# Moving the first head pair's projections ahead of the values' stage, and new ratios for merging attention with projections, in a one-core decoder layer

## The chip, the cores and the metric

One core of a Trainium2 chip runs the whole kernel. The metric is the time of one execution in device microseconds, the median of repeated runs; three runs of the kernel before took 2665.83, 2668.41 and 2672.25 us. One more execution was recorded by the hardware profiler, and all numbers of single instructions come from that one.

## The reference, cut to what matters

The layer takes a residual stream x of 1024 tokens by 1024 channels in float32 and applies four blocks, each with a norm ahead and behind: a SwiGLU feed-forward half, a mixer, a cross-attention to 256 memory tokens and a second feed-forward half. The change lies in the mixer, in its first half:

```
proj = u @ w_in
q, k, v, z, xs, bm, cm, dt_raw = split(proj)
# stick-breaking attention, 16 heads of 64, strictly causal:
zz = (q @ k.T) / 8
suffix = reverse_cumsum(log_sigmoid(-zz)) - log_sigmoid(-zz)
a = exp(log_sigmoid(zz) + suffix)          # s < t only
o_att = rmsnorm(a @ v)
# beside it a state-space scan of 16 heads over xs, bm, cm, dt gives o_ssd
m = concat([o_att, o_ssd]) @ w_out
```

## The kernel before

Float32 products are made on TensorE from a high part and a low part of each operand, three matmuls for one (line 279, `mm3`). A projection of one 128-column weight tile over one half of the tokens (512) is 8 x 3 matmuls (line 286, `proj`), accumulated in one bank of a PSUM pool "mm" of three.

**Order of the work.** TensorE's order is written out by hand: every matmul is made to follow the one that the program lists before it (line 100, `_pe`), and a clock of estimated costs runs along. Other engines follow their own lists, ordered by a scheduler that knows the program order as a priority. Some steps are put down with a due time on that clock (line 122, `run_later`) and are listed when TensorE's order has come that far. `merge` (line 156) interleaves two generators so that their shares of two given times, `ta` and `tb`, advance together.

**Weights** come through `wstream` (line 255), one tile ahead of its use: by a transfer on SP, from a copy already split in DRAM where there is one, or raw into "wraw" (two buffers) and then split by ScalarE (high part) and VectorE (low part). High and low parts have three buffers each. A transfer on SP that waits for a buffer holds up all behind it on that queue; POOL's queue works in the same way.

**The stage ahead** is the state-space scan (line 1188, `ssd`). Its last work is `keys` (line 1478), eight tiles of the memory's keys, whose results pass through a buffer "ko" of the tag "Bt" (one buffer) on their way to DRAM.

**Attention** (line 1578) begins with `value_rows` (line 1894): in two halves of the output columns, eight token blocks accumulate in eight PSUM banks at once over four weight tiles. At the end of a half ScalarE reads each bank out, POOL's queue shifts the block by one token, VectorE takes the difference of neighbours, both are split into a buffer of the tag "v" (four buffers), and POOL's queue stores it to DRAM. `differ` and `store` are listed 6.0 and 8.5 us after the block's matmuls on the planner's clock. In DRAM the values lie by head, so that a block's store writes pieces of 512 bytes.

Then the heads go in eight pairs. `inproj(p)` (line 1630) makes queries, keys and loads values of pair p: two projections for the queries (both token halves), two for the keys; each result is split and taken by small row transfers on SP (128 KB each) into operands where a head's high and low parts lie one above the other ("q", "k", and "QL" for the queries' low part). `units(p)` (line 1818) makes the products: for two heads and four groups of 256 queries, `scores` (line 1710: two matmuls per part, a sigmoid on ScalarE, a scan along the keys on VectorE), and one group later `values` (line 1812: transposes on TensorE, a split by ScalarE and VectorE into "ath" and "atl", four buffers each, and matmuls with the values, up to three behind). Pair 0's `inproj` runs alone; then each pair's `units` is merged with the next pair's `inproj`:

```
self.run_all(inproj(0))
for p in range(7):
    self.merge(units(p), 24000, inproj(p + 1), 32500)
self.merge(tail(), 26000, beside(), 21000 + 5200 * MIXED)
```

In the last `inproj`, `before` (line 1692) also loads and scales tiles of the scan's output for the output projection. `tail` is the last pair's products; `beside` is the first part of the output projection and then the memory's values. After that `mix_out` (line 1975) loads the attention's output ("oraw") and squares and sums it.

## Time and profile before

| | us |
|---|---|
| median of three runs | 2668.41 |
| profiled execution | 2669.86 |
| its span | 2667.9 |
| values' stage, first matmul after the keys to last | 1026.3 to 1116.8 |
| pair 0's projections, alone | 1116.8 to 1138.6 |
| products of pair 0 with projections of pair 1 | 1155.6 to 1201.7 |
| one pair of the middle | 50.3 |
| products of the last pair begin | about 1505 |

How to read it: the table's stages are read off the times at which the matmuls of each stage start. The profile gives each engine's busy time, the clock granted to TensorE and the share of the time in which the 16 DMA engines were busy. A row of a timeline has start, duration, engine, line of the code, operation, result and operands; in brackets stands the idle time of the engine just before it, and what ended it. A row of stretches has the length, then for TensorE, its weight loads, VectorE, ScalarE and POOL the busy time with the count of instructions, then granted clock, DMA share and GB/s. A row of DMA issues ends with the size of one and the median time from issue to landing. A row of waits has the total, the count and the longest.

### The profile page before, as it was taken

What the parts mean: (1) busy time and instruction counts of PE and PEld (TensorE: products, weight loads), DVE (VectorE), ACT (ScalarE), POOL (GpSimd) and SP (SyncE); (2) the same over time, 40 slices, a digit from 0 to 9 for tenths busy, and PEclk for the clock granted to TensorE, in tenths of its full rate; (3) what the DMA queues carried; (4) which work ended last, traced back from release to release, by engine and by line L of the source; (5) the groups of instructions that cost most, each with busy time, mean ns of one, the idle gap of its engine ahead of it and who ended that gap; (6) DMA issues with size and microseconds to landing.
All of it is one profiled execution on the core that took longest, in us unless ns stands there. A gap on an engine that the chain in (4) does not pass through costs nothing.

```text
span 2667.9 us, 36670 instructions
## 1 busy us (share of the span) xinstructions
PE 2592.1 (97%) x12786; PEld 2152.1 (81%) x12786; DVE 1941.8 (73%) x2928; ACT 1289.4 (48%) x2232; POOL 662.8 (25%) x822
## 2 busy tenths in 40 slices
PE   9899999999999999979999999999999999999999
PEld 7788888778777788868888787888878788888887
DVE  6778897778689783357777776767565888776767
ACT  6434444555356563345565555346554433333554
POOL 2555553110100001412222210101011555552000
PEclk9999999999999999989999999999999999999999
DMA  6458888774655223775554646637648443236554
GB/s 224 163 193 276 284 282 293 261 248 164 229 184 180 87 79 123 224 193 130 145 148 119 178 129 225 219 128 241 225 150 298 164 166 127 89 105 217 193 166 155
DMA packets 211049, 493.74 MB, mean 185 GB/s; under 512 B 27568, under 2 KB 35888, under 8 KB 210864
## 3 DMA queue, kind: packets, MB, share of 16 engines
q1 hardware_dynamic: 155408, 357.42, 40.2%
q0 software_dynamic: 32128, 91.51, 11.4%
q10 hardware_dynamic: 23328, 42.48, 4.2%
q8 instruction: 100, 1.64, 0.2%
q14 instruction: 85, 0.70, 0.1%
HBM read 327.46 MB, written 138.67 MB: 175 GB/s over the span
## 4 chain that ended last, share of the span: by engine, by line
PE 67%; issue 16%; DVE 7%; DMA 6%; ACT 2%; POOL 1%; SPq 1%; DVEq 0%; ACTq 0%; POOLq 0%
PE mm L138 32%; PE dn L138 28%; PE z L138 2%; DVE nb L1730 1%; PE tr L141 1%; PE ms L138 1%; PE ms L141 1%; PE tr L138 1%; DMA wraw<-in_w_dn 1%; DMA raw<-xs 1%; DMA raw<-in_w_dn 1%; DVE atl L1783 1%; DVE hl L267 1%; DMA oraw<-mix 1%; DMA wraw<-xs 0%
## 5 line engine op out<-in xcount | busy, mean ns | idle before, releaser
L138 PE MATMUL mm<-xh,whi 128*128 128x512 f32 x1192 | 469.9, 404 | 3.9 <-ACT xh L265 2.7
L138 PE MATMUL mm<-xl,whi 128*128 128x512 f32 (+1 forms) x1124 | 438.9, 390 | 5.4 <-DVE xl L267 4.2
L138 PE MATMUL mm<-xh,wlo 128*128 128x512 f32 x1144 | 439.0, 392 | 0.0
L138 PEld LDWEIGHTS mm<-xh,whi 128*128 128x128 f32 x1192 | 225.4, 189 | 45.4 <-ACT xh L265 3.9
L138 PEld LDWEIGHTS mm<-xh,wlo 128*128 128x128 f32 x1144 | 215.3, 188 | 46.8 <-DVE wlo L267 0.4
L138 PEld LDWEIGHTS mm<-xl,whi 128*128 128x128 f32 x1124 | 212.7, 189 | 39.5 <-DVE xl L267 6.3
L1730 DVE TENSOR_TENSOR_SCAN nb<-nb,begin 128x128 f32<-128x128 f32 (+7 forms) x128 | 169.9, 1350 | 52.6 <-ACT nb L1726 52.3
L267 DVE TENSOR_TENSOR wlo<-wraw,whi 128x1024 fp32r<-128x1024 f32 x78 | 95.2, 1221 | 85.1 <-ACT whi L265 84.8
L265 ACT CAST whi<-wraw 128x1024 fp32r<-128x1024 f32 (+1 forms) x95 | 92.3, 972 | 112.8 <-PE mm L138 54.5
L1726 ACT ACTIVATE nb<-z,scale 128x128 f32<-128x128 f32 (+2 forms) x192 | 106.1, 582 | 68.4 <-PE z L138 68.1
L657 ACT ACTIVATE ft<-ft 128x512 f32<-128x512 f32 x88 | 55.5, 632 | 101.1 <-DVE ft L656 100.5
L138 PE MATMUL dn<-xh,wlo 128*128 128x512 f32 x296 | 101.3, 390 | 0.0
L740 POOL TENSOR_TENSOR wc<-wraw,raw 128x512 f32<-128x512 f32 x56 | 80.3, 1434 | 65.1 <-DVE whi L267 17.9
L1782 ACT ACTIVATE ath<-tr,small 128x512 fp32r<-128x512 f32 (+1 forms) x106 | 68.2, 645 | 57.2 <-PE tr L141 53.9
L740 POOL TENSOR_TENSOR wc<-raw,wraw 128x512 f32<-128x512 f32 x55 | 81.1, 1475 | 51.5 <-DVE blk L267 21.6
L138 PE MATMUL z<-k,q 128*128 128x128 f32 (+2 forms) x192 | 67.1, 353 | 26.0 <-DMA k<-dg 16.9
L1783 DVE SCALAR_TENSOR_TENSOR atl<-tr,ath 128x512 fp32r<-128x512 f32 (+1 forms) x106 | 65.7, 625 | 36.2 <-ACT ath L1782 35.4
L825 POOL TENSOR_TENSOR ft<-ft,e 128x512 f32<-128x512 f32 x37 | 59.7, 1614 | 121.4 <-DVE e L824 45.1
L138 PE MATMUL mm<-ath,v 128*128 128x256 f32 x320 | 89.2, 301 | 0.1
L138 PE MATMUL dn<-xh,blk 128*128 128x512 f32 x264 | 85.2, 389 | 0.0
L138 PE MATMUL mm<-atl,v 128*128 128x256 f32 x320 | 83.5, 283 | 0.5 <-DVE atl L1783 0.5
L265 ACT CAST wlo<-wc 128x512 fp32r<-128x512 f32 x79 | 49.1, 621 | 70.8 <-PE dn L138 28.1
(602 smaller groups left out, 6992.2 us busy)
## 6 DMA issues: line engine op xcount, KB each, us to landing
whi<-dwhi SPq DMA_DIRECT2D x74, 512.0 KB, 3.6
wlo<-dwlo SPq DMA_DIRECT2D x74, 512.0 KB, 4.7
wraw<-in_w_gu SPq DMA_DIRECT2D x43, 512.0 KB, 3.9
raw<-in_w_gu SPq DMA_DIRECT2D x37, 512.0 KB, 4.1
wraw<-xs SPq DMA_DIRECT2D x56, 256.0 KB, 3.0
xs<-ft ACTq DMA_DIRECT2D x54, 256.0 KB, 3.3
raw<-xs SPq DMA_DIRECT2D x54, 256.0 KB, 3.2
act<-ft ACTq DMA_DIRECT2D x52, 256.0 KB, 2.3
```

Of the source, the lines that this page charges most:

```text
L138: self._pe(self.nc.tensor.matmul(out, lhsT, rhs, start=start, stop=stop, skip_group_check=self.more), cost)
L141: self._pe(self.nc.tensor.transpose(out, src, self.ident if ident is None else ident), 109.0)
L265: self.kp(self.nc.scalar.copy(hi, src))
L267: self.nc.vector.tensor_tensor(out=lo, in0=src, in1=hi.bitcast(F32), op=ALU.subtract)
L657: nc.scalar.activation(t, t, AF.Silu)
L740: nc.gpsimd.tensor_tensor(out=t, in0=a, in1=b, op=op)
L825: nc.gpsimd.tensor_tensor(out=t1, in0=t1, in1=e, op=ALU.mult)
L1726: nc.scalar.activation(nb[:, s0:s1], z[:, 0:n], AF.Sigmoid, scale=sc[:, i : i + 1])
L1730: nc.vector.tensor_tensor_scan(out=nb[:, 0:Wd][:, ::-1], data0=nb[:, 0:Wd][:, ::-1], data1=begin[:, S - Wd : S][:, ::-1], initial=0.0, op0 ...
L1782: nc.scalar.activation(hi, x, AF.Identity, bias=self.minus)
L1783: nc.vector.scalar_tensor_tensor(out=lo, in0=x, scalar=-1.0, in1=hi.bitcast(F32), op0=ALU.add, op1=ALU.subtract)
```

## The change

- The weight stream hands out query tile 0 and key tile 1 of the first pair ahead of the values' tiles, and key tile 1 again behind them.
- `inproj(0)` makes the queries and the first half of the keys, then calls `value_rows`, then makes the second half of the keys with the tile that came again. The value buffers of a pair are taken when they are loaded. The second set of "QL" is made and cleared behind the values.
- The values lie in DRAM by token block: a block's store writes whole rows of 4 KB, and a head's load reads pieces of 512 bytes. Blocks 5 to 7 are read out into "ath" and "atl" buffers instead of "k".
- The last two tiles of the memory's keys use the tag "csr" instead of "Bt".
- `merge` gets other times: 24900 (20240 for pair 0) to 20740 (21600 for the last), and 32500 for the tail.
- The tiles that `before` loads have two buffers of their own ("mraw"), and a load is listed two steps ahead of its use; the last projection gives way once more before its end.

```diff
--- before.py
+++ after.py
@@ -1491,7 +1491,7 @@
                         nc.vector.tensor_tensor(out=t, in0=ps, in1=rm, op=ALU.mult)
                     i = n % 2
                     if i == 0:
-                        env["ko"] = self.t(sp, [P, 4, MEM], F32R, "Bt")
+                        env["ko"] = self.t(sp, [P, 4, MEM], F32R, "Bt" if n < 6 else "csr")
                     o = env["ko"]
                     self.split(o[:, i, :], o[:, 2 + i, :], t)
                     if i == 1:
@@ -1500,7 +1500,8 @@
             env = {}
             W = self.W = self.wstream(
                 [self.wsrc("ssd", i % 6 if i < 12 else i) for i in range(26)] + [self.wsrc("kv", i) for i in range(8)]
-                + [ap["w_v"][i] for i in range(8)] + [self.wsrc("qk", i) for i in range(16)]
+                + [self.wsrc("qk", i) for i in range(2)] + [ap["w_v"][i] for i in range(8)]
+                + [self.wsrc("qk", i) for i in range(1, 16)]
             )
 
             def inproj():
@@ -1596,16 +1597,19 @@
                     out=sc[:, 4 * hh : 4 * hh + 4], in0=self.C[hh], scalar1=-0.125, scalar2=None, op0=ALU.mult
                 )
             W = self.W
-            V_d = self.value_rows(sp, pp, W)
+            V_d = []
             Wm = self.wstream([self.wsrc("kv", 8 + i) for i in range(8)])
             heads = {}
 
 
             QLs = []
-            for pool, tag in ((self.wp, "wraw"), (sp, "ql")):
+
+            def new_QL(pool, tag):
                 QLs.append([self.t(pool, [P, S], F32R, tag, bufs=2) for _ in range(2)])
                 for a, x in enumerate(QLs[-1]):
                     nc.gpsimd.memset(x[64 - a * 64 : 128 - a * 64, :].bitcast(F32), 0.0)
+
+            new_QL(sp, "ql")
 
 
             spare = [self.xl(hh, F32R) for hh in range(2)]
@@ -1630,8 +1634,7 @@
             def inproj(p):
                 Q = [self.t(sp, [P, S], F32R, "q", bufs=3) for _ in range(2)]
                 K = [self.t(sp, [P, S], F32R, "k", bufs=3) for _ in range(2)]
-                V = [self.t(sp, [P, 8, P], F32R, "v", bufs=4) for _ in range(2)]
-                QL = QLs[p % 2]
+                V, QL = [], QLs[p % 2]
                 heads[p] = (Q, K, V, QL)
 
                 def evac(ps, hh):
@@ -1641,7 +1644,8 @@
                     return t
 
                 def fetch(a):
-                    (nc.sync if p else nc.gpsimd).dma_start(out=V[a].bitcast(F32), in_=V_d[p // 4][:, 2 * (p % 4) + a].bitcast(F32))
+                    V.append(self.t(sp, [P, 8, P], F32R, "v", bufs=4))
+                    (nc.sync if p else nc.gpsimd).dma_start(out=V[a].bitcast(F32), in_=V_d[p // 4][:, :, 2 * (p % 4) + a].bitcast(F32))
 
                 def qevac(ps, sl):
 
@@ -1668,6 +1672,8 @@
                     wk = next(W)
                     kevac(evac((yield from self.proj(wk, 0)), 0), h0)
                     if not p:
+                        V_d.extend(self.value_rows(sp, pp, W))
+                        new_QL(self.wp, "wraw")
                         fetch(0)
                     fetch(1)
                 else:
@@ -1681,21 +1687,26 @@
                             before(n // 2)
                         yield
                     qevac((yield from last), h1)
+                if not p:
+                    wk = next(W)
                 last = self.proj(wk, 1)
-                for n in range(6):
+                for n in range(7):
                     next(last)
                     if p == 7:
                         before(3 + n)
                     yield
                 kevac(evac((yield from last), 1), h1)
 
+            raws = []
+
             def before(n):
 
                 if n < 8:
-                    k = n
-                    raw = self.t(sp, [P, H], F32, "ev", bufs=2)
-                    nc.sync.dma_start(out=raw, in_=self.mix_d[8 + k][:, 0:H])
-                    self.scaled_split(self.XH[0][k], self.XL[0][k], raw, self.par("ssd_norm_g", k))
+                    raws.append(self.t(wsp, [P, H], F32, "mraw", bufs=2))
+                    nc.sync.dma_start(out=raws[n], in_=self.mix_d[8 + n][:, 0:H])
+                if n > 1:
+                    k = n - 2
+                    self.scaled_split(self.XH[0][k], self.XL[0][k], raws[k], self.par("ssd_norm_g", k))
                 if n == 2:
                     ready.append(next(self.Wo))
                 if n == 6:
@@ -1885,8 +1896,8 @@
             wo = [self.wsrc("out", 8 * part + d) for n in range(2) for part in (1, 0) for d in range(8)]
             self.Wo, self.mix_r, ready, late = self.wstream(wo[0:MIXED]), [], [], []
             for p in range(7):
-                self.merge(units(p), 24000, inproj(p + 1), 32500)
-            self.merge(tail(), 26000, beside(), 21000 + 5200 * MIXED)
+                self.merge(units(p), 24900 if p else 20240, inproj(p + 1), 20740 if p < 6 else 21600)
+            self.merge(tail(), 32500, beside(), 21000 + 5200 * MIXED)
             self.Wo = self.wstream(wo[MIXED:])
             with self.pinned(self.clock + 2500):
                 vout(*pend_v.pop(0))
@@ -1894,7 +1905,7 @@
     def value_rows(self, sp, pp, W):
 
         nc = self.nc
-        V_d = [self.tc.dram_tile([P, 8, KT, P], F32R, name=self.nm("v")) for _ in range(2)]
+        V_d = [self.tc.dram_tile([P, KT, 8, P], F32R, name=self.nm("v")) for _ in range(2)]
         rows = {}
 
         def at(t, f, *args):
@@ -1916,7 +1927,7 @@
             self.split(o[:, :, 0:64], o[:, :, 64:128], y)
 
         def store(n, tb):
-            self.kp(nc.gpsimd.dma_start(out=V_d[n][:, :, tb].bitcast(F32), in_=rows.pop((n, tb)).bitcast(F32)))
+            self.kp(nc.gpsimd.dma_start(out=V_d[n][:, tb].bitcast(F32), in_=rows.pop((n, tb)).bitcast(F32)))
 
         for n in range(2):
             ps = [self.t(self.mmp, [P, H], F32, "mm") for _ in range(3)]
@@ -1933,10 +1944,13 @@
                         self.mm3(ps[tb], [(self.XH[hh][k][:, c], self.XL[hh][k][:, c], *b)], k == 0, k == 7)
                     if q < 3:
                         continue
-                    x = self.t(sp, [P, 2, H], F32, *(("nb", 5), ("k", 3))[tb > 4])
-                    rows[tb] = x[:, 0], x[:, 1]
+                    if tb < 5:
+                        x = self.t(sp, [P, 2, H], F32, "nb", bufs=5)
+                        rows[tb] = x[:, 0], x[:, 1]
+                    else:
+                        rows[tb] = [self.t(sp, [P, H], F32, tag, bufs=4) for tag in ("ath", "atl")]
                     with self.urgent():
-                        nc.scalar.activation(x[:, 0], ps[tb], AF.Copy, scale=self.C[hh][:, tb % 4 : tb % 4 + 1])
+                        nc.scalar.activation(rows[tb][0], ps[tb], AF.Copy, scale=self.C[hh][:, tb % 4 : tb % 4 + 1])
                     at(600, shift, tb)
                     at(6000, differ, n, tb)
                     at(8500, store, n, tb)
```

## The prediction

> **What bounds the kernel now.** I read the page first, then the idle times of TensorE in order of time, then the waits and the DMA rows around each long one. All times are of the profiled execution.
>
> ```profile
> span 2667.9 us, 36670 instructions
> PE 2592.1 (97%) x12786; PEld 2152.1 (81%) x12786; DVE 1941.8 (73%) x2928; ACT 1289.4 (48%) x2232; POOL 662.8 (25%) x822
> ```
>
> TensorE is busy for 97% of the span and the change takes no matmul away, so all it can win is idle time of TensorE and clock lost after it. In the stage that the change touches one stretch stands out:
>
> ```profile
> 1138.32 0.39 PE L138 MATMUL mm<-xh,wlo 128*128 128x512 f32 x1
> 1155.57 0.44 PE L138 MATMUL z<-k,q 128*128 128x128 f32 x1 [16.86 <-DMA k<-dg]
> 1117.00:1157.00 40.00, 23.14 (x101) 18.91 (x100) 11.93 (x19) 8.26 (x13) 10.53 (x16) 0.81 0.98 278
> 1155.50:1162.00 6.50, 6.43 (x26) 5.55 (x27) 2.58 (x4) 2.59 (x5) 0.00 (x0) 0.73 1.02 275
> ```
>
> The last projection of pair 0 starts at 1138.32, the first score matmul at 1155.57: 16.86 us idle, released by a row of keys. In the two rows of stretches the last three numbers are granted clock, DMA share and GB/s. The DMA engines were full (0.98) for the whole 40 us, and after the gap the clock stood at 0.73 for 6.5 us, which loses 6.5 x 0.27 = 1.75 us more. What the DMA engines were full of:
>
> ```profile
> 1116.56 0.39 PE L138 MATMUL ms<-whi,xl 128*128 128x512 f32 x1
> 1135.93 0.85 POOL L1919 DMA_DIRECT2D v<-v  x1 [0.88 <-DVE v L267]
> 1136.69 0.64 POOL L1644 DMA_DIRECT2D v<-v  x1
> 1146.78 0.72 SPq L1628 DMA_DIRECT2D k<-dg  x1
> v<-v POOLq DMA_DIRECT2D x18, 512.0 KB, 7.0
> q<-xl SPq DMA_DIRECT2D x4, 128.0 KB, 10.1
> k<-dg SPq DMA_DIRECT2D x2, 128.0 KB, 7.9
> ACT v L265 <- DMA v<-v: 6.6, 3, 2.9
> ACT v L265 <- DMA k<-k: 2.1, 1, 2.1
> ```
>
> The values' matmuls end at about 1116.8, but their eight blocks of the second half are stored until 1135.93, 19.1 us later. Each store takes 7.0 us to land, and ScalarE, which must split the next block into one of four "v" buffers, waits 6.6 us in three pieces for landings. Pair 0's query and key rows queue into the same full engines (10.1 and 7.9 us to land). So here the end is set by DMA behind the values, not by TensorE.
>
> **The change part by part.**
>
> *Queries and first half of keys in front of the values, second half behind.* TensorE does the same work in another order. The rows of both query halves and of the first key half, 12 + 4 transfers of 128 KB, now land while the values' 84 us of matmuls run. The first scores need only these, so the 16.86 us and the clock behind them go: -18.6 us. Key tile 1 is loaded a second time, two transfers of 512 KB; they fall into
>
> ```profile
> 1100.00:1110.00 10.00, 10.00 (x46) 8.27 (x45) 0.00 (x0) 1.38 (x2) 1.24 (x3) 1.00 0.31 116
> ```
>
> a stretch whose DMA share is 0.31, ahead of the last stores, and cost nothing there. Without that cover 1 MB at the 278 GB/s of the full stretch would be 3.8 us.
>
> What is late next: the tail of the values itself. TensorE now has one projection behind them (24 matmuls, three in 0.68 us by the starts around 1138: 5.4 us), not four, and then scores, whose sigmoids queue on ScalarE behind the splits that wait for landings. The loads of pair 0's values are written before the last blocks' splits and can take two of the four "v" buffers; blocks 5 to 7 now wait in the "ath" and "atl" buffers that the first transposes want. Before does not show this overlap, so I bound it. Below: 0, if the stores land sooner without the rows beside them. Above: 19.1 + 7.0 - 5.4 = 20.7 us, if nothing of the pair runs until the last store has landed. I take ScalarE's own waits of before, 6.6 + 2.1 = 8.7 us, the row of the same instructions. In the same place POOL has the two loads issued ahead of the stores rather than behind them, and the two clearing writes of the second "QL" set move behind the values; both are under 1 us each and wait for nobody.
>
> *Whole rows.* Stores now write 4 KB per partition and the sixteen loads read 512-byte pieces; before it was the reverse. Equal bytes, equal counts; I give it 0 on TensorE.
>
> ```profile
> 1080.00:1100.00 20.00, 20.00 (x90) 16.55 (x89) 7.06 (x10) 3.44 (x5) 8.24 (x10) 1.00 0.96 271
> 1600.00:1620.00 20.00, 19.41 (x109) 16.66 (x108) 11.76 (x20) 11.30 (x20) 5.76 (x12) 1.00 0.90 300
> ```
>
> The stretch of the first half's stores moved 271 GB/s at a share of 0.96, or 282 at a full one; a stretch of 256 and 512 KB loads moved 300 at 0.90, or 333. The Trainium skill, "DMA: Bandwidth & Descriptors", Specifications, has line rate from 512 bytes on, so by it whole rows bring the stores nothing and the 8.7 stays; by the two rows a store would land in 7.0 x 282 / 333 = 5.9 us, an estimate, the three waits would be 3.3 us shorter, and the sum below -31.2.
>
> *The "csr" buffer and the seam to the values.*
>
> ```profile
> 1032.34 0.50 PE L138 MATMUL mm<-whi,xh 128*128 128x512 f32 x1 [1.69 <-DVE sq L1491]
> ```
>
> The values open three "mm" banks at once and met one that was not yet read out. A projection opens one at a time, 5.4 us apart, and the last keys no longer wait for an earlier store's buffer: -1.7 us, between 0 and 1.7.
>
> *The merge by counts.* With the planner's costs (0.422 ns a column, 109 a transpose, 213 for a short matmul) a pair's products count 24.9 us and a projection set 20.74. At 24000 to 32500 the projections are used up when products stand at 20.74 x 24 / 32.5 = 15.3, and the last 9.6 run alone. There the idle times sit, in each pair the same three:
>
> ```profile
> 1294.15 0.44 PE L138 MATMUL z<-k,q 128*128 128x384 f32 x1 [0.44 <-ACT nb L1726]
> 1298.10 0.50 PE L138 MATMUL z<-k,q 128*128 128x512 f32 x1 [0.43 <-ACT nb L1726]
> 1304.10 0.66 PE L141 MATMUL ms<-ident,nb 128*128 128x128 f32 x4 [0.34 <-DVE atl L1783]
> 1198.02 0.50 PE L138 MATMUL z<-k,q 128*128 128x512 f32 x1 [0.96 <-ACT nb L1726]
> 1252.00:1302.30 50.30, 49.09 (x298) 42.31 (x297) 36.16 (x43) 29.92 (x57) 12.86 (x31) 1.00 0.52 137
> ```
>
> Five pairs lose 1.21 us each, pair 0 0.96: 7.0 us. With projections up to the end each score has 1.8 times the time, and VectorE's 36.16 us per pair stay below TensorE's 49.09: -7.0 us, between 0 and 7.0.
>
> *The border to the last pair.* Here the same stall meets loads of the state-space output, which ScalarE scales in order:
>
> ```profile
> 1489.59 2.61 SPq L1697 DMA_DIRECT2D ev<-mix  x2
> 1495.49 0.72 ACT L272 ACTIVATE xh<-ev,params 128x512 fp32r<-128x512 f32 x1 [3.90 <-DMA ev<-mix]
> 1498.09 0.44 PE L138 MATMUL z<-k,q 128*128 128x384 f32 x1 [2.93 <-ACT nb L1726]
> 1499.61 0.44 PE L138 MATMUL z<-k,q 128*128 128x384 f32 x1 [0.44 <-ACT nb L1726]
> 1504.83 0.44 PE L138 MATMUL z<-k,q 128*128 128x384 f32 x1 [0.48 <-ACT nb L1726]
> 1513.88 0.88 PE L141 MATMUL tr<-ident,nb 128*128 128x128 f32 x3 [2.33 <-DVE nb L1730]
> 1495.00:1515.00 20.00, 13.82 (x72) 11.02 (x71) 18.35 (x22) 14.96 (x30) 6.97 (x16) 0.89 0.74 219
> ```
>
> Idle 2.93 + 0.44 + 0.48 + 2.33 = 6.2 us, clock 20 x 0.11 = 2.2. The loads get buffers of their own and are written two steps ahead, so ScalarE's 3.90 us should go. I leave the 2.33, a scan that came late: -6.1 us, between 0 and 8.4. The Trainium skill, "TensorE: Matmul & The Clock Gate", Part 1, lets the clock fall after about 3.4 us without work; by that the 2.93 us would cost no clock and the sum would be -25.7, an estimate. The row's 0.89 speaks against it.
>
> *The end of attention.*
>
> ```profile
> 1631.01 1.84 PE L138 MATMUL ms<-small,asum 128*128 128x1 f32 x8 [3.01 <-DVE asum L1993]
> 1630.00:1640.00 10.00, 8.99 (x36) 7.71 (x37) 8.79 (x14) 7.37 (x10) 0.00 (x0) 0.66 0.71 256
> ```
>
> The tail counts 29.6 us, the work beside it 54.6. At 26000 to 52200 the tail had 2.4 us left alone; at 32500 it ends with 7.1 us of the other left. So the attention output, whose sum of squares TensorE waits for here (3.01 us and 10 x 0.34 = 3.4 of clock), is stored earlier, but its loads may still wait for memory that the work beside holds until its end. Between 0 and 6.4; no row is nearer to one end, so half: -3.2 us.
>
> **Sum:** -18.6 + 8.7 - 1.7 - 7.0 - 6.1 - 3.2 = -27.9 us. The profiled execution took 2669.86 us, 1.45 above the median shown; 2669.86 - 27.9 = 2642.0.
>
> **The rivals.**
>
> *The stage's tail moves into pair 0 whole.* The new wait is 20.7, not 8.7: 2654.0, and 2665 where the two last terms and the seam bring nothing either. For it: ScalarE runs in order, and buffers are fewer. Against: no rows beside the stores.
>
> *The wait moves ahead of the values.* If the first values' weights queue on SP behind the second queries' six rows:
>
> ```profile
> 1284.49 0.59 SPq L1628 DMA_DIRECT2D k<-dg  x1
> wraw<-in_w_v SPq DMA_DIRECT2D x3, 512.0 KB, 3.4
> 1006.82 1.23 DVE L267 TENSOR_TENSOR wlo<-wraw,whi 128x1024 fp32r<-128x1024 f32 x1 [0.54 <-ACT whi L265]
> ```
>
> two passes of some 0.7 us each over the queries, 6 x 0.59, 3.4 to land, two passes of some 1.2 over the weights: 10.7 us against one projection's 5.4, so 5.3 us more: 2647.3. Against it: SP has nothing else then, and these loads were issued early in before.
>
> *Slower: the last key half comes too late at every border.* With exact counts a pair's last projection ends together with its products, and the next pair's third score group reads these keys. Between lie 0.64 + 3.36 + 0.76 + 0.76 = 5.5 us of products, 10.1 with the projections beside them.
>
> ```profile
> 1290.76 0.68 DVE L1640 TENSOR_TENSOR ev<-mm,rpre 128x512 f32<-128x512 f32 x1
> 1292.12 2.48 SPq L1628 DMA_DIRECT2D k<-xl  x4
> k<-xl SPq DMA_DIRECT2D x20, 128.0 KB, 3.2
> ```
>
> Now the rows are there at 1292.12 + 2.48 + 3.2 = 1297.8, 7.0 us after the projection: 3 us to spare. If they landed as slowly as in the full stretch (10.1), each of seven borders would stall 3.8 us and lose 1.75 of clock: 39 us, and the kernel takes 2681. It decides from 4.0 us per border on.
>
> *It does not do what it says:* the products' order on TensorE is written out, so the merge happens; that the values' loads come after the stores as before would hold the first product up, and is part of the first rival.
>
> **How the numbers follow.** Forecast 0.53; tail moved whole 0.20, of which 0.06 near 2665; wait ahead of the values 0.14; late keys 0.10; all of it won and no new wait (-42, 2628 and below) 0.03. The range leaves out the last two: 2627 to 2665. About 0.2%, 5.3 us, is what a measurement of this kernel can tell from no change. Faster 0.53 + 0.14 + 0.14 + 0.03 = 0.84, same 0.06, slower 0.10.
>
> **What would show it.** Right: no idle time over 5 us between the values and the first score, key rows landed before the values end, ScalarE's waits for "v" landings around the first scores summing to some 9 us; idle times below 0.3 us inside pairs 1 to 5; no wait for the loads of the state-space output. Wrong: TensorE idle for DMA just ahead of the values' first matmul, or at the third score group of each pair, or the 16.86 us back under another name behind the values.

## The result, and the profile after

The changed kernel takes 2655.96 us (five runs, 2654.68 to 2659.27) against 2666.79 us of the kernel before on the same chip (2665.03 to 2672.25): a ratio of 0.9959 [0.9944, 0.9973]. It is faster, by 10.8 us or 0.4%, and the interval leaves out 1; 27.9 us were forecast. The profiled executions differ by 13.9 us, because the one of before lay 3 us above its median. The page of the kernel after:

```profile
span 2654.0 us, 36652 instructions
PE 2590.9 (98%) x12786; PEld 2153.6 (81%) x12786; DVE 1940.4 (73%) x2928; ACT 1290.0 (49%) x2232; POOL 658.2 (25%) x822
```

The work is the same, so the difference lies in the gaps. To place it I cut both traces at the same rows of TensorE: the first matmul behind the memory's keys, the first score of each pair ("z", 128 columns), the first matmul of the output projection. Two such rows of after:

```profile
1135.74 0.22 PE L138 MATMUL z<-k,q 128*128 128x128 f32 x1
1194.01 0.22 PE L138 MATMUL z<-k,q 128*128 128x128 f32 x1
```

Between them lies pair 0: 1194.01 - 1135.74 = 58.27 us. All segments in this way (us, in brackets the idle time of TensorE that the trace lists in it):

| segment | before | after | difference | forecast |
|---|---|---|---|---|
| code ahead, unchanged | 1026.26 | 1024.19 | -2.1 | 0 |
| pair 0's projections and values, to its first score | 129.31 (18.55) | 111.55 (0) | -17.8 | -18.6 |
| pair 0 | 46.11 (0.96) | 58.27 (10.36) | +12.2 | +6.0 |
| pairs 1 to 5 | 251.14 (5.73) | 249.66 (5.04) | -1.5 | -6.1 |
| pair 6, with the border to the last | 56.62 (4.19) | 50.18 (0.43) | -6.4 | -6.1 |
| last pair and tail, to the output projection | 108.35 (4.54) | 111.25 (7.27) | +2.9 | -3.2 with the next |
| from there to the end | | | -1.2 | |

The forecast column holds the terms of the prediction where their time lies: the gap and the seam less the lost clock (-16.86 - 1.69) in the second row; the clock, the new wait and pair 0's share of the merge (-1.75 + 8.7 - 0.96) in the third. The unchanged code ahead begins the stage anywhere between 1022.5 and 1029.2 us over all the profiles of this study, so its -2.1 means nothing. Other segments differ between profiles too, where the code does not: TensorE's order is the same in e9 and e10 below up to the last pair, and yet pair 0 differs by 1.5 us and pair 6 by 2.4; the five traces with the new tail time (after, e1, e3, e5, e6) have 107.8 to 111.4 us for the last pair and tail. A single difference of under some 3 us in one segment says little.

**What was won.** The 16.86 us ahead of the first score are gone, and the border to the last pair is clean. The seam was moved rather than removed: of the two waits of before (the second stands in the prediction) one is left, at the first projection. Before's other row, then after's:

```profile
1026.26 0.77 PE L138 MATMUL mm<-whi,xh 128*128 128x512 f32 x1 [0.98 <-DVE sq L1491]
```

```profile
1024.19 0.80 PE L138 MATMUL mm<-xh,whi 128*128 128x512 f32 x1 [2.03 <-DVE sq L1491]
```

Before waits 0.98 + 1.69 = 2.67 us there, after 2.03.

**What came back.** TensorE's idle times in pair 0, and the stretches around them (clock, DMA share and GB/s are the last three numbers):

```profile
1146.35 0.55 PE L138 MATMUL z<-k,q 128*128 128x256 f32 x1 [4.80 <-DMA k<-xl]
1152.63 0.86 PE L141 MATMUL tr<-ident,nb 128*128 128x128 f32 x3 [2.95 <-DVE nb L1741]
1163.23 0.63 PE L141 MATMUL tr<-ident,nb 128*128 128x128 f32 x4 [1.92 <-DVE atl L1794]
1135.74:1194.01 58.27, 47.78 (x255) 39.93 (x254) 38.79 (x47) 30.31 (x55) 14.89 (x33) 0.94 0.74 220
1140.00:1145.00 5.00, 1.54 (x9) 1.06 (x7) 0.50 (x1) 1.63 (x3) 3.10 (x6) 1.00 1.06 293
1145.00:1150.00 5.00, 3.33 (x10) 2.77 (x10) 0.00 (x0) 0.47 (x1) 0.00 (x0) 0.66 1.02 269
```

VectorE did 0.50 us of work in one five-microsecond stretch and none in the next. What it stood at, from its timeline, POOL's, ScalarE's and SP's, and the row of DMA issues:

```profile
1132.36 0.94 POOL L1648 DMA_DIRECT2D v<-v  x1
1138.35 2.48 SPq L1632 DMA_DIRECT2D k<-xl  x4
1139.79 0.90 POOL L1648 DMA_DIRECT2D v<-v  x1 [6.28 <-DMA v<-v]
1140.68 0.56 POOL L1916 DMA_DIRECT2D atl<-ath  x1
1150.28 0.69 DVE L1924 TENSOR_TENSOR atl<-atl,ath 128x512 f32<-128x512 f32 x1 [9.78 <-DMA atl<-ath]
1151.40 0.62 ACT L265 CAST v<-nb 128x512 fp32r<-128x512 f32 x1 [3.78 <-DMA v<-v]
k<-xl SPq DMA_DIRECT2D x4, 128.0 KB, 7.2
```

Read from the top: pair 0's first load of values takes one of the four "v" buffers at 1132.36. Its second load (1139.79) has no buffer and holds POOL's queue for 6.28 us until a store has landed. The last block's shift (L1916) is the next entry of that queue, so it starts at 1140.68. The subtraction that needs it (L1924) stands in VectorE's order ahead of the scans of the first scores, 9.78 us. Beside it the rows of the second key half land only in time for 1146.35.

**Inside a pair** two waits are left, here pair 1's, with the stretch of the pair. The first is shown with the two score steps just before it: three in a row, and the scores have two banks.

```profile
1205.17 0.34 PE L138 MATMUL z<-k,q 128*128 128x384 f32 x1
1205.52 0.28 PE L138 MATMUL z<-k,q 128*128 128x256 f32 x1
1206.49 0.44 PE L138 MATMUL z<-k,q 128*128 128x384 f32 x1 [0.57 <-ACT nb L1737]
1231.32 0.45 PE L138 MATMUL z<-k,q 128*128 128x384 f32 x1 [0.43 <-ACT nb L1737]
1194.00:1244.00 50.00, 48.99 (x300) 42.82 (x298) 36.41 (x43) 30.15 (x56) 13.38 (x32) 1.00 0.55 137
```

**At the end of attention** new waits stand where before had one of 1.72 and one of 0.49 us: for the single "ms" bank, for weights, and for attention rows that are read back. The last of them lies behind the start of the output projection.

```profile
1555.61 0.90 PE L141 MATMUL ms<-ident,nb 128*128 128x128 f32 x3 [3.17 <-ACT sq L353]
1594.28 0.50 PE L138 MATMUL mm<-xh,wlo 128*128 128x512 f32 x1 [1.90 <-DMA wlo<-dwlo]
1614.32 0.72 ACT L272 ACTIVATE ohi<-oraw,params 128x512 fp32r<-128x512 f32 x1 [4.02 <-DMA oraw<-mix]
1615.09 0.51 PE L138 MATMUL dn<-ohi,whi 128*128 128x512 f32 x1 [3.04 <-ACT ohi L272]
1555.00:1619.00 64.00, 57.88 (x375) 52.61 (x376) 37.34 (x57) 32.21 (x56) 8.64 (x18) 0.96 0.71 230
```

### The profile page after: what moved, and what is told of

Same layout as the page of the kernel before. It is cut to its first block, busy times and chain, and to the rows that moved or that the text cites. A ratio compares the mean times of both kernels' runs of the same rounds, so it can differ in the third digit from the quotient of the medians.

```text
span 2654.0 us, 36652 instructions
## 1 busy us (share of the span) xinstructions
PE 2590.9 (98%) x12786; PEld 2153.6 (81%) x12786; DVE 1940.4 (73%) x2928; ACT 1290.0 (49%) x2232; POOL 658.2 (25%) x822
## 5 line engine op out<-in xcount | busy, mean ns | idle before, releaser
L1793 ACT ACTIVATE ath<-tr,small 128x512 fp32r<-128x512 f32 (+1 forms) x109 | 70.3, 646 | 53.3 <-PE tr L141 47.2
L1773 POOL DMA_DIRECT2D mix<-o x60 | 49.7, 828 | 151.1 <-DMA mix<-o 130.0
L138 PE MATMUL dn<-xh,whi 128*128 128x512 f32 x240 | 83.2, 391 | 0.0
```

What stands on the lines that cost most here:

```text
L138: self._pe(self.nc.tensor.matmul(out, lhsT, rhs, start=start, stop=stop, skip_group_check=self.more), cost)
L1773: nc.gpsimd.dma_start(out=out, in_=x, accum_op=ALU.add)
L1793: nc.scalar.activation(hi, x, AF.Identity, bias=self.minus)
```

## The experiments

Theory A: the stall in pair 0 is made by buffers and by queues worked in order. Rival B: the DMA engines are full, and whatever is late there is late in any order. Theory C: the waits inside pairs come from score steps that follow each other. Segments of all runs, in us with the idle time; the medians are of four runs or more, and the kernel before took 2665.7 to 2667.4 us beside them.

| kernel | median | ratio to before | pair 0 | pairs 1 to 5, each | pair 6 | last pair and tail |
|---|---|---|---|---|---|---|
| after | 2655.96 | 0.9959 [0.9944, 0.9973] | 58.27 (10.36) | 49.9 (1.0) | 50.18 | 111.25 (7.27) |
| e1 late load | 2652.59 | 0.9941 [0.9928, 0.9954] | 52.53 (6.25) | 49.9 (1.0) | 50.66 | 108.43 (5.88) |
| e2 old merge times | 2650.30 | 0.994 [0.9927, 0.9954] | 54.18 (7.02) | 50.2 (1.1) | 51.98 | 106.36 (3.97) |
| e3 old layout | 2657.85 | 0.9961 [0.9948, 0.9974] | 56.23 (9.53) | 49.9 (1.0) | 50.52 | 107.80 (5.37) |
| e4 old tail time | 2648.63 | 0.9933 [0.9922, 0.9945] | 57.38 (8.95) | 49.9 (1.0) | 50.25 | 104.16 (2.20) |
| e5 keys ahead | 2653.61 | 0.9952 [0.9937, 0.9967] | 61.50 (11.38) | 49.9 (1.0) | 50.51 | 111.39 (6.21) |
| e6 five buffers | 2656.53 | 0.9958 [0.9946, 0.997] | 53.81 (6.70) | 49.9 (1.0) | 53.76 | 110.87 (5.82) |
| e7 three parts | 2643.49 | 0.9913 [0.99, 0.9926] | 53.09 (6.74) | 50.0 (1.1) | 50.00 | 104.26 (2.21) |
| e8 spaced | 2634.52 | 0.9876 [0.9861, 0.9891] | 52.77 (7.09) | 48.1 (0) | 50.68 | 104.42 (2.21) |
| e9 six buffers | 2633.29 | 0.9881 [0.9863, 0.9898] | 53.28 (6.31) | 48.1 (0) | 50.73 | 104.53 (2.20) |
| e10 spaced tail | 2636.02 | 0.9883 [0.9869, 0.9897] | 51.81 (6.11) | 48.1 (0) | 53.14 | 104.05 (2.20) |
| e11 before, spaced | 2666.04 | 0.9999 [0.999, 1.0008] | 46.60 (1.33) | 50.2 (1.1) | 53.28 | 108.29 (4.68) |
| e12 late stores | 2636.25 | 0.9893 [0.9876, 0.9909] | 52.43 (6.67) | 48.1 (0) | 51.13 | 104.46 (2.20) |

### The stall in pair 0: e1, e5, e6

e1 moves the second load of pair 0's values behind the second key half:

```diff
                         fetch(0)
-                    fetch(1)
+                    else:
+                        fetch(1)
...
                 kevac(evac((yield from last), 1), h1)
+                if not p:
+                    fetch(1)
```

> The changed kernel, but pair 0's load of the second head's values is written behind the second key half, not right after the values' stage. Theory A (a jam on POOL's queue): in the changed kernel that load stands on POOL's queue for 6.3 us waiting for a value buffer, the last block's shift stands behind it, and VectorE, in order, stands 9.8 us waiting for the shift; the scans come late. Then VectorE's 9.8 us wait falls below 3 us, of TensorE's idle 4.8 + 3.0 + 1.9 us around the first scores at least 5 go, and the kernel is 5 to 9 us faster than the changed one, near 2649 us. Theory B (full DMA engines alone): the key rows are late because of the bytes in flight; 0.5 MB less ahead of them at about 290 GB/s is 1.8 us, the rest of the idle time stays, and the kernel is 1 to 3 us faster, near 2654 us.

Pair 0 lost 5.7 us, as A has it, and VectorE's longest wait there fell from 9.78 to 3.39 us. It is not the whole stall, though, and the median fell by 3.4 us only, between the two forecasts. What is left in the trace of e1:

```profile
1142.34 0.62 ACT L265 CAST v<-nb 128x512 fp32r<-128x512 f32 x1 [6.97 <-DMA v<-v]
1144.69 0.44 PE L138 MATMUL z<-k,q 128*128 128x384 f32 x1 [3.98 <-ACT nb L1740]
1151.65 0.35 PE L138 MATMUL z<-k,q 128*128 128x256 f32 x1 [1.58 <-DMA k<-xl]
```

Now it is ScalarE whose split waits for a "v" buffer, 6.97 us, with the first sigmoids behind it: the wait that the prediction had taken for the whole.

e5 puts all four projections of pair 0 ahead of the values (the weight stream hands out key tile 1 once, and `inproj(0)` ends with the values):

```diff
                     if not p:
+                        kevac(evac((yield from self.proj(wk, 1)), 1), h1)
                         V_d.extend(self.value_rows(sp, pp, W))
...
                 if not p:
-                    wk = next(W)
+                    return
```

> All four projections of pair 0 stand ahead of the values, so the second key half's rows have long landed and nothing but the values' tail is left in pair 0. Theory A (the stall is made by four value buffers and by queues worked in order: the second load of values on GpSimd's queue ahead of the last shift, VectorE and ScalarE standing behind them): the values and their stores now end one projection, 5.4 us, later with nothing between them and the scores, so TensorE's idle time between the first score and the second pair grows from 10.4 to about 15 us, and the whole is some 4 us slower than the changed kernel, near 2660. Theory B (the full DMA engines bring the keys too late): the 4.8 us at the third score group go, and with four row transfers fewer in the full stretch the rest shrinks too; idle 5.6 us or less, near 2651.

The keys' wait went and the idle time did not fall (11.4 us against 10.4), which speaks against B as it was put; but it did not grow to 15 us either, so A had the price of the moved projection too high. Nor were the engines full around its longest idle time, 3.39 us up to 1157.26: the DMA share is 0.75 from 1150 to 1155 and 0.54 from 1155 to 1160. The median equals that of after within its interval; the profiled execution lay 10 us above it, so its segments are the weakest of the table.

e6 gives the values five buffers. The loads of the state-space output pay for it and go back to the two shared "ev" buffers, at their old place:

```diff
-                    V.append(self.t(sp, [P, 8, P], F32R, "v", bufs=4))
+                    V.append(self.t(sp, [P, 8, P], F32R, "v", bufs=5))
...
-            o = rows[n, tb] = self.t(sp, [P, KT, P], F32R, "v", bufs=4)
+            o = rows[n, tb] = self.t(sp, [P, KT, P], F32R, "v", bufs=5)
...
-                    raws.append(self.t(wsp, [P, H], F32, "mraw", bufs=2))
-                    nc.sync.dma_start(out=raws[n], in_=self.mix_d[8 + n][:, 0:H])
-                if n > 1:
-                    k = n - 2
+                    k = n
+                    raw = self.t(sp, [P, H], F32, "ev", bufs=2)
+                    nc.sync.dma_start(out=raw, in_=self.mix_d[8 + k][:, 0:H])
```

> Value buffers five instead of four; to make room the loads of the state-space output go back to the two shared buffers and their old place. The two parts show at different places. Theory A: GpSimd's 6.3 us and VectorE's 9.8 us go, pair 0 takes 51 to 54 us instead of 58.3, and only the key rows' wait stays. Theory B: same bytes in the same full engines, so the splits wait for landings as before and pair 0 stays at 57 to 58 us. At the border to the last pair: if the buffers of their own made the cure, pair 6 takes 53 to 56 us again (before: 56.6, changed: 50.2, changed with old merge times: 52.0); if not, 50 to 51.

Both parts answered at their own place, and together they cancel in the median. Pair 0 falls to 53.8 us: A's number. Not only the key rows' wait stays, however, as A had it: ScalarE's split waits 6.85 us for a landing, as in e1. Pair 6 goes back to 53.8 us, with this wait, which the buffers of their own had removed:

```profile
1480.55 0.53 PE L138 MATMUL z<-k,q 128*128 128x384 f32 x1 [2.71 <-ACT nb L1736]
```

### The times of the merges: e2, e4, e11

e2 gives back all merge times, e4 the tail's alone:

```diff
-                self.merge(units(p), 24900 if p else 20240, inproj(p + 1), 20740 if p < 6 else 21600)
-            self.merge(tail(), 32500, beside(), 21000 + 5200 * MIXED)
+                self.merge(units(p), 24000, inproj(p + 1), 32500)
+            self.merge(tail(), 26000, beside(), 21000 + 5200 * MIXED)
```

```diff
-            self.merge(tail(), 32500, beside(), 21000 + 5200 * MIXED)
+            self.merge(tail(), 26000, beside(), 21000 + 5200 * MIXED)
```

> The changed kernel with all merge times as before (24000 to 32500, tail 26000), so that the new order, the whole rows and the loads in buffers of their own stand alone. If the merge times saved what the record says (7.0 us inside the pairs), it is some 5 to 7 us slower than the changed kernel. If, as its trace suggests, the stall inside a pair only moved (1.0 us in place of 1.2), the pairs give back 1 to 2 us; the tail, which got 2.9 us longer under the new times, gives 3 us the other way, and the kernel is within 3 us of the changed one. At the border to the last pair: if the loads' buffers cured it, the 2.93 us wait stays away; if the merge did, 3 to 6 us of idle time come back there.

> The changed kernel with the tail's merge time at 26000 again, all else as changed. From the start of the last pair's products to the first matmul of the output projection proper, the kernel before took 108.4 us and the changed one 111.3. If the new tail time costs that, this run is 2 to 4 us faster than the changed kernel. If it won what the record says (3.2 us), this run is 3 us slower; if neither, within 1 us.

The tail's time alone costs 111.25 - 104.16 = 7.1 us, and the medians say the same, 2655.96 - 2648.63 = 7.3, where 2 to 4 were expected. With the old time the waits for the "ms" bank, the weights and the rows read back are all gone; 1.72 and 0.48 us stay, as before. One wait went the other way: the one for the attention output's sum of squares, which the prediction named with 3.01 us, is gone under the new time and is back here with 2.74. The same 64 us in e4's trace, against the last row of the fence on the end of attention:

```profile
1548.30 0.38 PE L138 MATMUL ms<-ident,cmem 128*128 128x128 f32 x1 [1.72 <-DVE atl L1794]
1613.15 1.84 PE L138 MATMUL ms<-small,asum 128*128 128x1 f32 x8 [2.74 <-DVE asum L2007]
1548.00:1612.00 64.00, 61.15 (x414) 55.96 (x414) 44.56 (x64) 36.89 (x64) 10.05 (x23) 1.00 0.71 224
```

TensorE starts 414 matmuls in it rather than 375. e2 is 5.7 us faster than the changed kernel, which neither of its expectations had. In it the old ratio of pairs 1 to 5 costs only 1.4 us for all five, and old times in pair 0 are 4 us better than the exact counts by these two traces; that they put more projections beside the scores that wait there is a guess, and pair 0's time was not tried by itself. Pair 6 stays cured in e2 (52.0 against 56.6 of before).

e11 is the kernel before with one rule in `merge`, that of e8 below.

> The kernel before with nothing but the rule that a projection step follows each score step while there is one. Theory C (score steps in a row on two banks): little is won, since here the projections are used up early under 24000 to 32500 and the rule takes them up still earlier; more scores run alone at the end of a pair, idle 1.2 us a pair or more, 50 to 51 us, 2665 to 2672. Rival E (the exact counts add nothing, the rule alone does it): pairs 1 to 5 fall to 48.1 us as with exact counts, 11 us in all, near 2655.

Nothing: 0.9999 [0.999, 1.0008], with pairs at 50.2 us. The rule is worth nothing while the projections run out early.

### Score steps in a row: e7, e8

e7 joins three parts: the late load of e1, old merge times in pair 0, and the old time of the tail.

```diff
-                self.merge(units(p), 24900 if p else 20240, inproj(p + 1), 20740 if p < 6 else 21600)
-            self.merge(tail(), 32500, beside(), 21000 + 5200 * MIXED)
+                self.merge(units(p), 24900 if p else 24000, inproj(p + 1), (20740 if p < 6 else 21600) if p else 32500)
+            self.merge(tail(), 26000, beside(), 21000 + 5200 * MIXED)
```

> Three parts together: the second load of pair 0's values behind the second key half, old merge times in pair 0, old time for attention's end; the rest as changed. If the gains of the single parts add where they lie at different places: pair 0 at 50 to 53 us (one part alone 52.5, the other 54.2: both take from the same 10.4 us), last pair with its tail at 104.2 us: 2655.96 - 6.5 - 7.1 = about 2642. Theory B would leave pair 0 at 54 us or more, near 2645.

2643.49 us. The tail's gain comes whole; in pair 0 the two parts take from the same stall and do not add.

e8 is e7 with one rule more: each score step of the first seven pairs gives way to a projection step.

```diff
-            i = 0 if live[0] and (not live[1] or ca * tb <= cb * ta) else 1
+            i = 0 if live[0] and (not live[1] or ca * tb <= cb * ta and not z) else 1
...
-                next((a, b)[i])
+                z = next((a, b)[i])
...
-                        if s1 < Wd:
-                            yield
+                        if s1 < Wd:
+                            yield p < 7
```

(The last step of a score tile yields the same value, and `z` is cleared ahead of each step.)

> As the run before it, and in the first seven pairs each step of scores is followed by a step of a projection as long as there is one. Theory C (the two waits of 0.43 and 0.57 us that a pair keeps come from two or three score steps in a row on two score banks, which exact counts put there because short score steps count little): idle in each of pairs 1 to 5 falls from 1.0 to under 0.3 us, a pair takes 49.2 us instead of 49.9, five to six pairs give 4 us. Rival D (ScalarE or VectorE is late in any order): the idle time stays near 1 us or moves to the transposes, 49.9 us or more.

C holds, with more than it promised. Pair 2 in e7, then in e8:

```profile
1250.26 0.44 PE L138 MATMUL z<-k,q 128*128 128x384 f32 x1 [0.57 <-ACT nb L1740]
1237.76:1287.70 49.94, 48.93 (x298) 42.75 (x297) 36.32 (x43) 30.18 (x57) 13.87 (x32) 1.00 0.54 138
```

```profile
1236.27:1284.38 48.11, 48.11 (x299) 42.69 (x297) 36.42 (x43) 30.68 (x56) 13.88 (x33) 1.00 0.58 144
```

Idle time in the pair is 0, and the pair takes 48.11 us, 1.83 less where the trace had listed 1.0 as idle. The other 0.8 us had been counted as busy (48.93 against 48.11). In which matmuls it lay is not shown: those with which a step of a projection begins (mm<-xh,whi) fall from a mean of 428 to 400 ns, but the value products mm<-ath,v rise from 298 to 320.

### What is left of pair 0: e9, e10, e12

e9 is e8 with two lent buffers for blocks 3 and 4 of the values' second half; the second "QL" set, which lives there, is made when pair 1 begins.

```diff
-            o = rows[n, tb] = self.t(sp, [P, KT, P], F32R, "v", bufs=4)
+            spare = n and 2 < tb < 5
+            o = self.t(self.wp, [P, KT, P], F32R, "wraw", bufs=2) if spare else self.t(sp, [P, KT, P], F32R, "v", bufs=4)
+            rows[n, tb] = o
```

> As the run with spaced scores (2634.52 us, pair 0 52.8 us with 7.1 us idle), but blocks 3 and 4 of the second half are split into two buffers that lie free until pair 1, so that with the first load of values no block waits for an earlier store's landing. Theory A (the buffers are what the stage's tail costs): ScalarE's wait of 6.7 us for a landing goes, the first sigmoids start with the scores, and the 3.7 us of TensorE go with it; pair 0 takes 47 to 50 us, the whole is near 2630. Theory B (full DMA engines): the wait moves to the next landing, a shift or the keys' rows, and pair 0 stays at 52 us or more, 2634 or above.

Here pair 0 comes out as B has it. ScalarE's wait of 6.7 us goes, but pair 0 stays at 53.3 us:

```profile
1140.11 0.69 DVE L1930 TENSOR_TENSOR atl<-atl,ath 128x512 f32<-128x512 f32 x1 [1.86 <-DMA atl<-ath]
1141.46 0.71 PE L141 MATMUL tr<-ident,nb 128*128 128x128 f32 x3 [2.69 <-DVE nb L1747]
1142.66 0.62 ACT L267 CAST v<-atl 128x512 fp32r<-128x512 f32 x1 [3.79 <-DMA v<-v]
1145.34 0.55 PE L138 MATMUL z<-k,q 128*128 128x256 f32 x1 [1.25 <-DMA k<-xl]
1140.00:1145.00 5.00, 2.64 (x8) 1.82 (x8) 3.83 (x5) 1.57 (x3) 0.00 (x0) 0.67 1.03 416
```

The wait has gone on to the next landings, a shift, a store and the key rows, in a stretch with a DMA share of 1.03 and 416 GB/s.

e10 spaces the scores of the last pair too (the `p < 7` of e8 becomes `True`):

> As the run before it, with a step of the work beside it behind each score step in the last pair too. Theory C (score steps in a row cost idle time wherever they stand): the last pair with its tail loses up to its 2.2 us of idle time, 102 to 104 us instead of 104.4. Rival: there ScalarE and VectorE carry the memory's splits too, and products that come later delay the output projection: 105 us or more.

Pair and tail 104.05 us against 104.53, the median within the span of e9's runs: no difference. What idle time is left there, 1.72 and 0.48 us, waits for VectorE's part of the split ("atl") and not for a score bank, so the rule has nothing to take. Pair 6 is 2.4 us longer in this trace with the order of e9; that is the spread of the profiles.

e12 lists the stores of blocks 3 to 7 10 us later on the planner's clock, on e9:

```diff
-                    at(8500, store, n, tb)
+                    at(18500 if n and tb > 2 else 8500, store, n, tb)
```

> As the run with six buffers (2633.29 us, pair 0 53.3 us with 6.3 us idle), but the stores of the second half's blocks 3 to 7 are written some 10 us later, so that the first scores, the shifts of the last blocks and the rows of the second key half meet fewer of them in the DMA engines. Nobody needs these stores before pair 4. Theory B (what is left of the wait is full DMA engines): the shifts (6.4 us to land) and the key rows (8.8 us) land sooner, TensorE's idle time in pair 0 falls from 6.3 to under 4 us, pair 0 takes 49 to 51 us, the whole is near 2630. Theory A (buffers held and queues in order): the two lent buffers and the four others come free 10 us later, the second load of values and the last splits wait for them, idle time stays at 6 us or grows, 2633 or above.

Pair 0 takes 52.4 us with 6.7 us idle, no difference that one trace can show, and B's 49 to 51 us did not come. But on the chip the edit moved one store of the five later: block 4's starts 15.5 us behind pair 0's first score instead of 3.2. Block 3's starts at 2.7 in both, and those of blocks 5 to 7 at 16.1, 16.8 and 26.6 us, in e9 at 16.6, 17.1 and 26.7. So e12 takes 512 KB out of the stretch, and no more, and it decides little between A and B. In this trace the last shift still arrives late, and TensorE waits for the scan behind it:

```profile
1144.53 0.69 DVE L1930 TENSOR_TENSOR atl<-atl,ath 128x512 f32<-128x512 f32 x1 [2.62 <-DMA atl<-ath]
1145.88 0.55 PE L141 MATMUL tr<-ident,nb 128*128 128x128 f32 x3 [3.44 <-DVE nb L1747]
1140.00:1145.00 5.00, 1.49 (x6) 0.86 (x5) 1.77 (x3) 2.12 (x4) 0.00 (x0) 1.00 1.01 365
```

Whether fewer bytes there (the weights of pair 1 are loaded in the same stretch) or another way to shift would take the last 6 us was not tried.

### The layout: e3

```diff
-        V_d = [self.tc.dram_tile([P, KT, 8, P], F32R, name=self.nm("v")) for _ in range(2)]
+        V_d = [self.tc.dram_tile([P, 8, KT, P], F32R, name=self.nm("v")) for _ in range(2)]
...
-            self.kp(nc.gpsimd.dma_start(out=V_d[n][:, tb].bitcast(F32), in_=rows.pop((n, tb)).bitcast(F32)))
+            self.kp(nc.gpsimd.dma_start(out=V_d[n][:, :, tb].bitcast(F32), in_=rows.pop((n, tb)).bitcast(F32)))
```

(and the load's index the other way round)

> The changed kernel with the values stored by head again, in pieces of 512 bytes, and loaded in whole rows. If 512-byte pieces move at the line rate, nothing changes: within 1 us. If whole rows speed the stores up (estimate from the record: 1.1 us for each of the waits on a store's landing), the wait for value buffers behind the stage grows and the kernel is 2 to 5 us slower than the changed one.

0.9961 [0.9948, 0.9974] against 0.9959: no difference that can be measured in the time. The Trainium skill, "DMA: Bandwidth & Descriptors", Specifications, has full rate from 512 bytes on; the traces do not agree. The stretch of the first half's stores in whole rows (after), then in pieces of 512 bytes (e3):

```profile
1090.00:1098.00 8.00, 8.00 (x37) 6.63 (x36) 4.43 (x7) 1.74 (x3) 2.77 (x6) 1.00 0.97 357
1092.00:1100.00 8.00, 8.00 (x37) 6.60 (x36) 2.71 (x5) 1.77 (x4) 3.25 (x4) 1.00 0.95 260
```

At nearly the same share, whole rows moved 357 GB/s and pieces 260. The last three stores of that half land in 2.9 to 3.5 us in after and in 4.8 to 5.5 in e3. But TensorE is busy for the whole stretch in both, and behind the second half the faster rows shortened no wait that could be measured.

## Why the prediction was wrong

**The gap ahead of pair 0** was right in cause and size: 16.86 + 1.69 us of idle time left the second segment, which became 17.8 us shorter. **The border** was right too: -6.4 for -6.1, and e6, which takes back the buffers of their own and the earlier place of the loads, loses 3.6 us of it. **Whole rows** were worth the 0 that they were given, but by luck: the stores of the first half did land sooner, as the prediction's estimate from two rows had it, and it was the time that did not answer. The time lies in the range, but the change was forecast 17 us too large by the medians and 14 by the profiled executions, nearly all of it in three terms.

**The new wait was mis-sized: 8.7 us forecast, some 15 measured.** Pair 0 became 12.2 us longer although 0.96 of merge and 1.75 of clock were to leave it, so the wait is worth 12.16 + 0.96 + 1.75 = 14.9 us, of which 10.4 are listed as idle, 58.27 x 0.06 = 3.5 are clock and 1.0 has no place. The step that failed is "I take ScalarE's own waits of before ... the row of the same instructions". ScalarE waited 3.78 and 2.33 us for landings in the changed kernel, and 6.97 in e1, so a wait of that size was there; but the step took one engine's wait for the whole. It wrote that POOL's two loads ahead of the stores "wait for nobody" beside the clearing writes; the second load did wait, 6.28 us for a buffer (in before it had waited 2.56 us already, with nothing urgent behind it), and what stood behind it was not the store but the last shift, for which VectorE then held the scans 9.78 us. The row of before:

```profile
1139.89 0.55 POOL L1644 DMA_DIRECT2D v<-v  x1 [2.56 <-DMA v<-v]
```

e1, which moves that one load, is 5.7 us shorter in pair 0. Part of the same stall goes with pair 0's new merge time: e2, with the old one, has 54.2 us there, but beside the late load the old time wins nothing more (e7 53.1, e1 52.5). The cause of the rest, some 6 us of idle time, is open. In e9 and e12 it waits for landings at a DMA share above 1.0, which speaks for full engines; but e5's longest idle time fell at shares of 0.75 and 0.54, and e12, the run that was to empty the stretch, moved one store. The first rival named the place and had 20.7 us for it; the truth lies between.

**The merges inside pairs: -7.0 forecast, of it -6.1 in pairs 1 to 5, where -1.5 were measured.** The count was right that projections now last to the end (in pair 1 of the changed kernel the last one starts 1.0 us before the next pair's first score). The step that failed is "With projections up to the end each score has 1.8 times the time": an even share of costs is not an even spacing. A short score step costs little, so the merge lists two or three of them in a row, and on two score banks the third waits (1206.49 above). e8 shows it: with the spacing pairs 1 to 5 take 240.6 us against 251.1 of before, 2.1 us less each. e11 shows that exact counts are needed as well: the spacing alone gives nothing.

**The end of attention: -3.2 forecast, +1.7 measured** (+2.9 and -1.2; by the five traces with this time the first part lies between -0.6 and +3.0). "No row is nearer to one end, so half" left out the other side of zero. The wait that the prediction named did go, 3.01 us for the sum of squares, but the new time of the tail costs 7.1 us in all (e4). The rows of after name three waits that the old time does not have, for the memory's row product, for weights and for the rows read back; which of them is the first cause was not taken apart.

**The seam**, -1.7 forecast, gave 0.6: the wait moved to the first projection.

The third rival, late keys at every border, did not come: at the borders of pairs 1 to 6 no wait for keys is listed. Of the prediction's signs of being right, two held: between the values and the first score TensorE has no idle time at all, and the first key half's rows had landed by 1049. Two did not: ScalarE's landings made 6.1 us and not some 9, and inside pairs 0.57 and 0.43 us are left, not under 0.3. Of the last, no wait for the loads of the state-space output, half is true: ScalarE still waits up to 1.5 us for them, TensorE no longer. And a sign of being wrong came: idle time is back under another name behind the values, 10.4 us where 16.86 had been.

## What to carry to other kernels

When a stage's tail is pushed under the next stage, follow each queue entry behind the first instruction that may lack a buffer: here one load without a buffer held POOL's queue, through it a shift, through that VectorE and the scans, and the price was a chain, not the wait of one engine. When two streams are merged by costs, check the spacing of the steps that share a bank as well as the totals: the balanced order was worth 1.5 us in five pairs, and 10.6 with a rule against neighbours. A merge time that helps in one place need not help in the next: only the tail's was tried by itself here, and old ones for pair 0 and the tail with new ones between them, the spacing and a load behind the keys give 2634.5 us, 0.9876 [0.9861, 0.9891] of before.

## What the runs showed of the hardware

- The clock fell after an idle time shorter than 3 us. In e9 TensorE had 0.58 us idle, 1.4 us of work, then 2.69 us idle, and ran the next matmuls of 512 columns in 0.63 us instead of 0.39:

```profile
1137.35 0.50 PE L138 MATMUL z<-k,q 128*128 128x512 f32 x1 [0.58 <-ACT nb L1743]
1138.38 0.39 PE L138 MATMUL mm<-xh,wlo 128*128 128x512 f32 x1
1143.04 0.63 PE L138 MATMUL mm<-xl,whi 128*128 128x512 f32 x1
1144.00:1146.00 2.00, 0.76 (x4) 0.69 (x4) 1.58 (x3) 0.23 (x1) 0.92 (x1) 0.50 1.05 419
1148.00:1150.00 2.00, 2.00 (x11) 1.64 (x9) 0.14 (x1) 1.16 (x2) 1.32 (x2) 0.87 0.40 137
```

  The clock stands at 0.50 and is still at 0.87 from 1148 to 1150. The Trainium skill, "TensorE: Matmul & The Clock Gate", Part 1, lets it fall after an idle window of about 3.4 us; by this trace a shorter gap is enough. e10 has it with one gap alone, of 2.21 us, with TensorE busy and the clock at 1.00 in the twelve us before:

```profile
1454.68 0.50 PE L138 MATMUL mm<-xh,whi 128*128 128x512 f32 x1 [2.21 <-ACT o L1768]
1456.00:1458.00 2.00, 2.00 (x8) 1.71 (x8) 2.00 (x5) 1.35 (x4) 0.84 (x2) 0.50 0.42 90
```

- A busy TensorE hides waits: the spaced order took 1.83 us from a pair with 1.0 us of listed idle time.
- The time that POOL needs to issue a DMA went with the pieces, at equal bytes: a 512 KB store took 0.85 us in 512-byte pieces before (its row stands in the prediction) and takes 0.58 in whole rows, and the load of the same size went from 0.64 to 0.90 (the row at 1139.79 above). e3, with the old layout, has 0.84 and 0.54 again:

```profile
1131.79 0.58 POOL L1930 DMA_DIRECT2D v<-v  x1
```
